# A hybrid attention layer on one core: scale and shift as columns made by one-column products, and the start stage reordered

## The chip, the cores and the metric

The kernel runs on one core of one Trainium2 chip. A core has a matrix engine (TensorE, PE in the profile, with its weight loads shown as PEld), VectorE (DVE), ScalarE (ACT), GpSimd (POOL) and SyncE (SP, which here only issues transfers). Each takes its own instructions in order; semaphores tie them together. The metric is the device time of one execution in microseconds (us), lower is better: the median of several runs.

## The reference

One decoder layer on x of 2048 rows by 1024. What matters here is the start: a conditioning vector c gives a shift, a scale and a gate of 1024 numbers each, and the normalised x is multiplied and moved by them before one wide input projection.

```python
mod = jax.nn.silu(c) @ w_ada[l] + b_ada[l]
shift, scale, gate = jnp.split(mod, 3, axis=-1)
h = rms_norm(x, g_pre[l]) * (1.0 + scale[:, None, :]) + shift[:, None, :]
proj = h @ w_in[l]
qa, ka, va, fa, za, qb, kb, vb, zb = jnp.split(proj, split_points, axis=-1)
oa = forgetting_attention(qa, ka, va, fa + b_fgate[l]) * jax.nn.silu(za)
ob = sliding_window_sink_attention(rope(qb), rope(kb), vb, sinks[l]) * jax.nn.silu(zb)
y = jnp.concatenate([oa, ob], axis=-1) @ w_out[l]
x = x + gate[:, None, :] * rms_norm(y, g_post[l])
```

(Reshapes are left out. `forgetting_attention` is causal softmax attention with a cumulative log gate, 8 heads of 64; the other is attention over a window of 128 with sinks.)

## The kernel before, in words

x is held as 16 blocks of 128 rows, x0 to x15, and four of them make a chunk (`ci` 0 to 3, 512 rows). For each chunk the kernel makes `hT[ci]`, the transposed, normalised, scaled and shifted x as two f16 parts, a high one and a low one, in 8 slices `k` of 128 columns. All projections are then three f16 products per slice (high by high, high by low, low by high) into one of three PSUM banks `bk`.

The start stage (lines 463 to 680) has to come before any of that:

- `load_ada(half, k)` loads one of 16 blocks of `w_ada`, 128x1024 f32, 512 KB: half 1 gives the scale, half 0 the shift. A ring of 8 buffers holds them, so half 0 waits until half 1 has been used. x0 to x3 are loaded behind the third block of half 0, x4 to x7 behind the last.
- The scale and the shift are needed as columns: number p of slice k in partition p, column k. Before, `silu(c)` is spread over 128 columns (`silb`) and is the stationary operand; a block of `w_ada` streams past it in two products of 512 columns (`ada_pe`), which gives the same row in all partitions. Four of the 16 blocks go over VectorE instead (`ada_dve`, multiply and add into `acc`), and `ada_sum` adds them in by a product with ones. `ada_col` picks the column out of the row by the identity and a reduction on VectorE.
- `squares(ci)` (ScalarE) and `root(ci)` make the inverse root of the mean square of each row; for chunk 0 the root is made on VectorE, for the others three instructions are on VectorE and the rest on GpSimd. `normal(ci)` multiplies the rows by it: on ScalarE for chunk 0, on VectorE for the others.
- A bound on |h| over all columns (`bmx`, then its maximum over the partitions) sets a power of two `pH`, and with it the final multipliers `Gp` and `Shp`.
- `turn(ci, k)` transposes slice k of the chunk's four blocks on TensorE; `scaled` (ScalarE, line 441) applies `Gp` and `Shp` to give the f32 slice `hf` and, for even k, the high part; `split` (VectorE, lines 445 and 446) makes the rest. Odd slices get their high part by a cast on VectorE.

Behind the start stage stands a list of units (`punits`, a slice number each): 8 units of the projection `kb` for chunk 0, then 8 of `vb`, then `zb0`, and so on; `fill` emits them in order, and `at_slice(n, f)` emits f just ahead of unit n. `kb` unit k needs both parts of `hT[0]` slice k. TensorE works through these units, and through all heads of attention behind them, in the order of the list.

Two things set the order in which instructions stand on an engine. Each engine keeps about the order of the code, but the framework puts single instructions earlier where it takes their inputs to be ready. A transfer whose buffer nothing has used before has nothing to wait for and can stand far ahead. Transfers from SP and ACT also share eight counters in turn: a transfer waits until the last one on its counter has landed (`DMAHW0` to `DMAHW7` in the rows below).

## Time and profile before

| | us |
|---|---|
| median of 3 runs (1157.06 to 1159.82) | 1157.67 |
| profiled execution, its own time | 1157.8 |
| its span, first to last instruction | 1156.1 |
| TensorE busy in it | 1116.8 (97%) |
| VectorE, ScalarE, GpSimd busy | 930.5, 661.4, 207.5 |

A row of the timeline gives the start, the length, the engine, the line of the code, what is written and read, how many instructions are merged, and in brackets the idle time before it with what ended that. Rows of stretches give the busy time of each engine, then TensorE's granted clock as a share of full speed, the busy share of the transfer engines, and GB/s. A product of f32 operands is shown as two records, a transpose as one.

### The profile page before, as it was taken

The page shows a single profiled execution, that of the slowest core. Times are in us where ns is not written, and L with a number is a line of the kernel's source. Part 1 is how long each engine was busy: PE and PEld are TensorE (multiplying, and loading weights), DVE is VectorE, ACT ScalarE, POOL GpSimd, SP SyncE. Part 2 cuts the span into 40 slices and gives each one's busy share as a digit, 9 for nine tenths or more (in the row PEclk, how much of TensorE's full clock was granted, in tenths as well). Part 3 has the DMA queues.
Part 4 walks back from the last instruction along what each step waited for, and adds up shares of the span by engine and source line. Part 5 has one row for each costly group of instructions (what it writes and reads, how often), then busy time and mean ns, then how long its engine had stood idle before and what let it go on. Part 6 is the DMA issues. An engine that isn't in the chain of part 4 may idle for free. (4 is left out here: it accounts for less than half of the span.)

```text
span 1156.1 us, 25291 instructions
## 1 busy us (share of the span) xinstructions
PE 1116.8 (97%) x9869; PEld 656.3 (57%) x9869; DVE 930.5 (80%) x2137; ACT 661.4 (57%) x1150; POOL 207.5 (18%) x332
## 2 busy tenths in 40 slices
PE   5899999999999999999999999999999999999997
PEld 2475544577765866555555555555555555544444
DVE  7877468987888568788988899888888887878885
ACT  2876344654555421666757666666776778534332
POOL 1122134554556530010010110001000000000000
PEclk9899999999999999999999999999999999999999
DMA  9943355433243232442344342123311337686743
GB/s 333 336 116 72 87 78 96 97 63 90 52 92 88 58 87 58 73 108 29 80 64 87 84 67 70 38 49 76 45 43 34 91 101 206 140 225 197 199 135 109
DMA packets 123476, 120.10 MB, mean 104 GB/s; under 512 B 64948, under 2 KB 100828, under 8 KB 123356
## 3 DMA queue, kind: packets, MB, share of 16 engines
q1 hardware_dynamic: 112088, 85.69, 27.6%
q0 software_dynamic: 10832, 32.50, 13.5%
q8 instruction: 77, 1.26, 0.6%
q14 instruction: 43, 0.35, 0.1%
q10 hardware_dynamic: 436, 0.28, 0.1%
HBM read 64.75 MB, written 25.18 MB: 78 GB/s over the span
## 5 line engine op out<-in xcount | busy, mean ns | idle before, releaser
L1356 ACT ACTIVATE p<-sta,lift,scl_qk 128x1024 f32<-128x1024 f32 (+2 forms) x160 | 172.0, 1075 | 131.6 <-PE sta L1350 82.6
L351 PE MATMUL bk<-hT,wh_qk 128*128 128x512 f16 x768 | 194.7, 378 | 0.0
L1363 DVE TENSOR_TENSOR pha<-p,pha 128x1024 f16<-128x1024 f32 (+2 forms) x160 | 169.1, 1057 | 0.2 <-ACT pha L1360 0.2
L1303 DVE TENSOR_REDUCE a_m<-bk 128x1 f32<-128x512 f32 x192 | 130.4, 686 | 45.8 <-PE bk L1300 44.8
L1576 PE MATMUL bk<-wohl,oz 128*128 128x512 f16 x744 | 165.3, 379 | 1.1 <-DVE oz L1525 0.7
L1360 ACT ACTIVATE pha<-p 128x1024 f16<-128x1024 f32 (+2 forms) x160 | 148.1, 926 | 5.9 <-PE poa L1376 1.2
L1576 PEld LDWEIGHTS <-oz 128*128 128x128 f16 x744 | 71.9, 99 | 82.8 <-DVE oz L1525 1.8
L1376 PE MATMUL poa<-vt,pha 128*128 128x65 f16 x1088 | 116.1, 192 | 1.4 <-DVE pha L1363 1.2
L1373 PE MATMUL poa<-vt,pha 128*128 128x65 f16 x1088 | 116.6, 193 | 0.8 <-DVE ona L1382 0.7
L1375 PE MATMUL poa<-vt,pha 128*128 128x64 f16 x1088 | 116.6, 194 | 0.0
L351 PEld LDWEIGHTS <-wh_qk 128*128 128x128 f16 x768 | 72.1, 97 | 74.4 <-issue 2.1
L1349 PE MATMUL sta<-T 128*128 128x512 f16 (+1 forms) x320 | 110.9, 346 | 2.8 <-ACT p L1356 2.7
L1300 PE MATMUL bk<-T 66*128 66x512 f16 (+2 forms) x320 | 109.7, 348 | 2.4 <-DVE a_m L1303 1.9
L1373 PEld LDWEIGHTS <-pha 128*128 128x128 f16 x1088 | 101.5, 96 | 15.5 <-DVE ona L1382 1.9
L1350 PE MATMUL sta<-T 69*128 69x512 f16 (+1 forms) x320 | 109.8, 348 | 0.0
L1375 PEld LDWEIGHTS <-pha 128*128 128x128 f16 x1088 | 100.9, 97 | 11.4
L1376 PEld LDWEIGHTS <-pha 128*128 128x128 f16 x1088 | 100.8, 99 | 1.8 <-DVE pha L1363 1.7
L351 PE MATMUL bk<-hT,wh_za 128*128 128x512 f16 x384 | 99.7, 378 | 0.0
L369 PE MATMUL bk<-wh_va,hT 128*128 128x256 f16 x768 | 91.9, 273 | 0.0
L351 PE MATMUL bk<-hT,wh_zb 128*128 128x512 f16 x384 | 91.6, 379 | 0.2 <-DVE qc L754 0.2
L351 PE MATMUL bk<-hT,wh_qb 128*128 128x512 f16 x384 | 91.2, 379 | 0.0
L369 PEld LDWEIGHTS <-hT 128*128 128x128 f16 x768 | 73.3, 98 | 12.2 <-issue 2.1
(459 smaller groups left out, 1919.7 us busy)
## 6 DMA issues: line engine op xcount, KB each, us to landing
hT<-in_x_dram SPq DMA_DIRECT2D x20, 512.0 KB
wa<-in_w_ada_dram SPq DMA_DIRECT2D x16, 512.0 KB
z_d<-tz POOLq DMA_DIRECT2D x32, 256.0 KB, 3.0
T<-z_d SPq DMA_DIRECT2D x16, 512.0 KB
T<-stq SPq DMA_DIRECT2D x62, 128.0 KB
out_dram<-hT SPq DMA_DIRECT2D x15, 512.0 KB
xt<-in_x_dram SPq DMA_DIRECT2D x12, 512.0 KB
qs<-qf SPq DMA_DIRECT2D x80, 64.0 KB
```

The source lines that it names most:

```text
L351: PE.matmul(ps, whl[:, a, k, :], hT[ci][:, b, k, :], start=(k == 0 and n == 0), stop=(k == KT - 1 and n == 2))
L369: PE.matmul(ps[:, (u % 2) * 2 * P:(u % 2 + 1) * 2 * P], hT[ci][:, a, k, u * P:(u + 1) * P], wv[p][:, b, k, :], start=(k == 0 and n == 0), ...
L1303: V.tensor_reduce(m3[:, u, pc:pc + 1], mx[:, :w], axis=AX.X, op=ALU.max)
L1349: PE.matmul(self.st[:, o:o + w], T[:, 3, kb_], T[:, 1, qc], start=True, stop=False)
L1350: PE.matmul(self.st[:, o:o + w], T[0:XR, 2, kb_], T[0:XR, 0, qc], start=False, stop=not diag)
L1356: A.activation(self.p32[:, :self.w], self.st[:, :self.w], AF.Exp, scale=scl[f"qk{self.hd}"][:], bias=lift[:])
L1360: A.activation(self.ph[:, 0, :self.w], self.p32[:, :self.w], AF.Copy)
L1363: V.tensor_tensor(self.ph[:, 1, :self.w], self.p32[:, :self.w], self.ph[:, 0, :self.w], op=ALU.subtract)
L1373: PE.matmul(po[:, u, :], ph[:, 0, pq], vt[:, b, hd, 0:65], start=(self.first and n == 0 and u == 0), stop=False)
L1375: PE.matmul(po[:, u, 0:64], ph[:, 0, pq], vt[:, b, hd, 65:VW], start=False, stop=False)
L1376: PE.matmul(po[:, u, :], ph[:, 1, pq], vt[:, b, hd, 0:65], start=False, stop=(self.last and n == len(self.blocks) - 1))
L1576: PE.matmul(py, self.hl[:, i, k, :], w_slot(8 * j + k)[:, cc], start=(k == 0 and m_ == 0), stop=(k == KT - 1 and m_ == 2))
```

## The change

The scale and the shift are made as columns at once: a 128x128 piece of a `w_ada` block is the stationary operand and the column of `silu(c)` the moving one, so one product gives 128 numbers of the result as one column (`ada_col(half, k)`: 8 such products per block, all 16 blocks on TensorE). `silb`, the two `acc` and VectorE's part are gone. The maximum of the bound over the partitions is made by one product of ones with a diagonal matrix `dgb` and one reduction, in place of a transpose, a reduction and a second product. Two of the four normalisations of chunk 0 go to VectorE. The squares of x6 and x7 move between the turned slices, and with them `root(1)` behind slice 4. The normalisations of chunk 1, two of which stood behind the start stage and two ahead of units 13 and 14, now all stand ahead of units (8, 9, 12, 13).

```diff
@@ normal
-            if ci == 0:
+            if ci == 0 and u < 2:
                 A.activation(xt[t], xt[t], AF.Copy, scale=r)
             else:
                 V.tensor_scalar(xt[t], xt[t], r, None, op0=ALU.mult)
@@ the start stage
-        silb = st.tile([P, KT, P], F32, name="silb")
-        V.tensor_copy(silb[:], sil[:].unsqueeze(2).broadcast_to([P, KT, P]))
-        pm = {1: [ps_x.tile([P, CH], F32, tag="x", name="pm") for _ in range(2)], 0: [bk[1], bk[2]]}
-        acc = [st.tile([P, D], F32, name=f"acc{n}") for n in range(2)]
-        def ada_mm(half, lhsT, rows_, begin, end):
-            for n in range(2):
-                PE.matmul(pm[half][n][:], lhsT, rows_[:, n * CH:(n + 1) * CH], start=begin, stop=end)
...
-        def ada_col(half, dst):
...
+        def ada_col(half, k):
+            for j in range(KT):
+                PE.matmul(bk[2 - half][:, j:j + 1], wa[half, k][:, j * P:(j + 1) * P], sil[:, k:k + 1],
+                          start=(k == 0 and j == 0), stop=(k == KT - 1 and j == KT - 1))
...
-        for k in (0, 1, 3, 4, 6, 7):
-            ada_pe(1, k, k == 0)
-        for k in (2, 5):
-            ada_dve(1, k, k == 2)
+        for k in range(KT):
+            ada_col(1, k)
...
-        ada_pe(0, 3)
-        ada_pe(0, 5)
+        for k in range(KT - 1):
+            ada_col(0, k)
         squares(0)
-        scl0 = col8("scl0")
-        ada_col(1, scl0)
+        scl1 = col8("scl1")
+        V.tensor_tensor(scl1[:], bk[1][:, 0:KT], cols[:, 24:32], op=ALU.add)
...
         root(0)
         normal(0)
-        ada_dve(0, 4, False)
-        ada_dve(0, 6, False)
-        ada_pe(0, KT - 1)
-        ada_sum(0, True)
         w_low("kb", 0, 1)
         w_low("vb", 0, 1)
-        turned = [turn(0, k) for k in range(5)]
-        squares(1)
-        shf0 = col8("shf0")
-        ada_col(0, shf0)
+        turned = [turn(0, k) for k in range(2)]
+        ada_col(0, KT - 1)
+        turned += [turn(0, k) for k in range(2, 4)]
+        squares(1, (0, 1))
         shf = col8("shf")
-        V.tensor_tensor(shf[:], shf0[:], cols[:, 16:24], op=ALU.add)
+        V.tensor_tensor(shf[:], bk[2][:, 0:KT], cols[:, 16:24], op=ALU.add)
...
         V.tensor_reduce(bmx[:], bnd[:], axis=AX.X, op=ALU.max)
-        PE.transpose(bk[0][0:1, 0:P], bmx[:], ident[:])
-        turned += [turn(0, k, bk[k - 4]) for k in (5, 6)]
-        bm = st.tile([1, 1], F32, name="bm")
-        V.tensor_reduce(bm[:], bk[0][0:1, 0:P], axis=AX.X, op=ALU.max)
-        PE.matmul(bk[0][:, P:P + 1], ones[0:1, :], bm[:], start=True, stop=True)
-        pow2_floor(pH[:], bk[0][:, P:P + 1], "p2t")
+        dgb = st.tile([P, P], F32, name="dgb")
+        V.tensor_scalar(dgb[:], ident[:], bmx[:], 1.0e-30, op0=ALU.mult, op1=ALU.max)
+        PE.matmul(bk[0][:, 0:P], ones[:], dgb[:], start=True, stop=True)
+        turned += [turn(0, 4)] + [turn(0, k, bk[k - 4]) for k in (5, 6)]
+        bm = st.tile([P, 1], F32, name="bm")
+        V.tensor_reduce(bm[:], bk[0][:, 0:P], axis=AX.X, op=ALU.max)
+        V.tensor_scalar(pH[:].bitcast(I32), bm[:].bitcast(I32), 0x7F800000, None, op0=ALU.bitwise_and)
...
-        V.tensor_scalar(pfl[:], ipH[:], 0.5, None, op0=ALU.mult)
-        root(1)
         for k in range(KT):
             turned[k][0]()
             turned[k][1]()
             if k == 0:
                 turned.append(turn(0, 7))
+                V.tensor_scalar(pfl[:], ipH[:], 0.5, None, op0=ALU.mult)
+            if k in (1, 3):
+                squares(1, (2 + k // 2,))
+            if k == 4:
+                root(1)
...
-        normal(1, (0, 1))
         spread(0)
@@ the list of units
-    for u in (2, 3):
-        at_slice(11 + u, lambda u=u: normal(1, (u,)))
+    for u in range(4):
+        at_slice((8, 9, 12, 13)[u], lambda u=u: normal(1, (u,)))
```

How the order moves on three engines follows; the number behind a name is that of the buffer.

SP at the very start of the program, before (`rows` are c, the gains and the biases, `wa10` is block 0 of half 1):

```order
L473 DMA rows_147<-in_c_dram 8x128 [waits DVE_49]
L474 DMA rows_147<-in_g_pre_dram 8x128
L475 DMA rows_147<-in_b_ada_dram 24x128
L480 DMA wa10_161<-in_w_ada_dram 128x1024
L480 DMA wa11_163<-in_w_ada_dram 128x1024 [waits DMAHW1_49]
```

SP at the same place, now (`xt12` is x12, a block of chunk 3):

```order
L410 DMA xt12_643<-in_x_dram 128x1024
L473 DMA rows_147<-in_c_dram 8x128 [waits DVE_49]
L474 DMA rows_147<-in_g_pre_dram 8x128
L475 DMA rows_147<-in_b_ada_dram 24x128
L480 DMA wa10_161<-in_w_ada_dram 128x1024 [waits DMAHW1_49]
L480 DMA wa11_163<-in_w_ada_dram 128x1024 [waits DMAHW2_49]
```

With `silb` and `acc` gone the buffer of x12 is one that the start stage does not use, and its load went from behind x11 to the first place. In the built program it holds counter 1, so the first block of `w_ada`, which waited for nothing, now waits until x12 has landed.

TensorE in half 0 of the scale and shift, before (`px` is a transposed slice, `acc0` the part from VectorE):

```order
L514 MATMUL bk1_137<-wa05_274,silb_198 128x512
L514 MATMUL bk2_138<-wa05_274,silb_198 128x512
L514 MATMUL bk1_137<-wa07_278,silb_198 128x512
L514 MATMUL bk2_138<-wa07_278,silb_198 128x512
L514 MATMUL bk1_137<-acc0_202,ones_125 128x512
L514 MATMUL bk2_138<-acc0_202,ones_125 128x512
L435 MATMUL px_378<-ident_116,xt0_262 128x128
```

TensorE at the same place, now:

```order
L507 MATMUL bk2_138<-sil_126,wa03_314 128x1 x8
L507 MATMUL bk2_138<-sil_126,wa04_316 128x1 x8
L507 MATMUL bk2_138<-sil_126,wa05_318 128x1 x8
L507 MATMUL bk2_138<-sil_126,wa06_320 128x1 x8
L435 MATMUL px_457<-ident_116,xt0_306 128x128
L435 MATMUL px_457<-ident_116,xt1_308 128x128
L435 MATMUL px_457<-ident_116,xt2_310 128x128
L435 MATMUL px_457<-ident_116,xt3_312 128x128
L435 MATMUL px_463<-ident_116,xt0_306 128x128
L435 MATMUL px_463<-ident_116,xt1_308 128x128
L435 MATMUL px_463<-ident_116,xt2_310 128x128
L435 MATMUL px_463<-ident_116,xt3_312 128x128
```

Blocks 4 and 6, which VectorE had, are on TensorE now, and the eight transposes of two slices stand ahead of block 7, whose eight products follow the last row.

VectorE in the turned slices of chunk 0, before (`hT0` and `hf` are the slices, `hT3` holds x4 to x7 at that time, `rst` is the inverse root of chunk 1; its three VectorE instructions stood ahead of the first slice):

```order
L446 TENSOR_TENSOR hT0_107<-hf_441,hT0_107 128x512 [waits Activation_49]
L445 CAST hT0_107<-hf_485 128x512 [waits Activation_49]
L446 TENSOR_TENSOR hT0_107<-hf_485,hT0_107 128x512 [waits DVE_49]
L672 TENSOR_REDUCE mxs_128<-wr_zb0_284 128x1 [waits DMAHW0_49]
L179 TENSOR_SCALAR kap_kb_508<-w_pw_321,pH_113 128x1
L179 TENSOR_SCALAR kap_vb_510<-w_pw_328,pH_113 128x1
L754 SCALAR_TENSOR_TENSOR qc_597<-bk0_136,cosT_111 128x512 [waits DMAHW5_49,DMAHW3_49,DMAHW7_49,DMAHW1_49,Activation_49]
L675 TENSOR_SCALAR kf_127<-kap_vb_510 128x1 [waits DVE_49]
L429 TENSOR_SCALAR hT3_110<-hT3_110,rst_409 128x1024 [waits DMAHW4_49,Pool_49]
L429 TENSOR_SCALAR hT3_110<-hT3_110,rst_409 128x1024
```

VectorE at the same place, now:

```order
L446 TENSOR_TENSOR hT0_107<-hf_511,hT0_107 128x512 [waits Activation_49]
L101 TENSOR_SCALAR rs_v_555<-ss_489 128x4
L106 TENSOR_SCALAR rs_h_558<-rs_v_555 128x4 [waits DVE_49]
L107 TENSOR_SCALAR rs_y_557<-rs_h_558 128x4 [waits DVE_49]
L445 CAST hT0_107<-hf_516 128x512 [waits Activation_49]
L446 TENSOR_TENSOR hT0_107<-hf_516,hT0_107 128x512 [waits DVE_49]
L446 TENSOR_TENSOR hT0_107<-hf_521,hT0_107 128x512 [waits Activation_49]
L429 TENSOR_SCALAR hT3_110<-hT3_110,rst_490 128x1024 [waits DMAHW5_49,Pool_49]
L445 CAST hT0_107<-hf_537 128x512 [waits Activation_49]
L429 TENSOR_SCALAR hT3_110<-hT3_110,rst_490 128x1024 [waits DMAHW6_49]
L446 TENSOR_TENSOR hT0_107<-hf_537,hT0_107 128x512 [waits DVE_49]
L634 TENSOR_REDUCE mxs_128<-wr_zb0_328 128x1 [waits DMAHW1_49]
```

The root of chunk 1 now begins behind slice 4, and the first two normalisations of chunk 1, the first of which waits for GpSimd, stand ahead of the cast and the low part of slice 7, where they had stood behind both.

21 lines of the change are left out of this document (removed).

## The prediction

> **What bounds the kernel now.** First the slices of the page and a table of stretches (columns: PE, PEld, DVE, ACT, POOL busy, TensorE's clock, share of the transfer engines, GB/s):
>
> ```profile
> PE   5899999999999999999999999999999999999997
> 0.00:20.00 20.00, 10.75 (x20) 4.15 (x21) 12.24 (x28) 4.68 (x8) 5.40 (x14) 1.00 0.88 300
> 20.00:40.00 20.00, 15.71 (x39) 6.73 (x38) 17.69 (x42) 13.80 (x21) 0.92 (x1) 0.91 1.03 406
> 60.00:70.00 10.00, 10.00 (x81) 7.32 (x79) 8.45 (x21) 7.81 (x14) 4.71 (x13) 1.00 0.38 90
> ```
>
> From 60 us on TensorE is the bound nearly without a break, so a delay at its first long run of products moves the end by as much. Up to 40 us the transfers are full, at 406 GB/s. The change lies wholly in this start. TensorE's timeline there:
>
> ```profile
> 6.67 3.39 PE L514 MATMUL pm<-wa,silb 128*128 128x512 f32 x4 [1.98 <-DMA wa<-in_w_ada_dram]
> 30.29 5.26 PE L514 MATMUL bk<-wa,silb 128*128 128x512 f32 x8 [3.97 <-DMA wa<-in_w_ada_dram]
> 35.88 1.98 PE L514 MATMUL bk<-wa,silb 128*128 128x512 f32 x4 [0.33 <-DMA wa<-in_w_ada_dram]
> 39.41 2.35 PE L435 MATMUL px<-ident,xt 128*128 128x128 f32 x20
> 45.69 0.38 PE L351 MATMUL bk<-hT,wh_kb 128*128 128x512 f16 x1 [1.90 <-ACT hT L441]
> 54.24 0.59 PE L351 MATMUL bk<-hT,wh_kb 128*128 128x512 f16 x2 [0.32 <-DVE hT L446]
> ```
>
> Three marks follow: block 3 of half 0 is there at 30.29 and block 7 at 35.88 (transfer); the turned slices begin on ScalarE behind `Gp` and `Shp`; `kb` of chunk 0 ends at 54.24 + 0.59 = 54.83. I measure the change by this last mark. Between the marks VectorE and ScalarE lead:
>
> ```profile
> 41.52 0.17 DVE L646 TENSOR_TENSOR shf<-shf,cols 128x8 f32<-128x8 f32 x1
> 42.12 0.16 DVE L652 TENSOR_REDUCE bmx<-bnd 128x1 f32<-128x8 f32 x1
> 42.65 0.28 DVE L657 TENSOR_REDUCE bm<-bk 1x1 f32<-1x128 f32 x1 [0.36 <-PE bk L654]
> 43.83 0.16 DVE L89 TENSOR_SCALAR p2t<-bk 128x1 f32<-128x1 f32 x1 [0.90 <-PE bk L658]
> 44.02 0.15 DVE L90 TENSOR_SCALAR pH<-p2t 128x1 int32<-128x1 int32 x1
> 44.74 0.16 DVE L101 TENSOR_SCALAR rs_v<-ss 128x4 f32<-128x4 f32 x1
> 45.14 0.17 DVE L107 TENSOR_SCALAR rs_y<-rs_h 128x4 int32<-128x4 int32 x1
> 50.36 0.72 DVE L446 TENSOR_TENSOR hT<-hf,hT 128x512 f16<-128x512 f32 x1 [0.18 <-ACT hf L441]
> 51.03 0.43 DVE L445 CAST hT<-hf 128x512 f16<-128x512 f32 x1
> 53.50 0.69 DVE L446 TENSOR_TENSOR hT<-hf,hT 128x512 f16<-128x512 f32 x1
> 56.17 1.40 DVE L429 TENSOR_SCALAR hT<-hT,rst 128x1024 f32<-128x1024 f32 x2
> ```
>
> ```profile
> 25.15 1.06 ACT L417 ACTIVATE junk<-xt 128x1024 bf16<-128x1024 f32 x1 [4.88 <-DMA xt<-in_x_dram]
> 26.49 1.06 ACT L417 ACTIVATE junk<-xt 128x1024 bf16<-128x1024 f32 x1 [0.20 <-DMA xt<-in_x_dram]
> 42.15 0.19 ACT L417 ACTIVATION_READ_ACCUMULATOR junk<-hT 128x1 f32 x1
> 44.86 0.78 ACT L441 ACTIVATE hT<-px,Shp,Gp 128x512 f16<-128x512 f32 x1 [2.53 <-DVE pfl L665]
> ```
>
> The reader sees 3.34 us from `shf` (41.52) to the first turned slice (44.86), which I call t, and 9.97 us from t to the end of `kb`.
>
> **Part 1, transfers.** x12 is loaded first, and block 0 of half 1 is issued only when it has landed. One 512 KB transfer takes 26.49 - 25.15 = 1.34 us, the lower bound of the delay. The upper one comes from the first block now:
>
> ```profile
> 2.22 0.36 SPq L480 DMA_DIRECT2D wa<-in_w_ada_dram  x1
> ```
>
> It was used at 6.67, 4.45 us behind its issue. If x12 is issued near 0.8 (an estimate: it stands ahead of the three small transfers that go first now) and takes as long, block 0 goes out at 5.25 in place of 2.22: 3.0 us late. In that gap the loads of `kb` and `vb` fill the engines, so I take 1.8, nearer the lower end: block 3 at 32.1, block 7 at 37.7. That x12 need not be loaded later costs and gives nothing I can see.
>
> **Part 2, one-column products.** A block is 8 products, 16 records. The nearest rows are a series of transposes, which load a 128x128 f32 operand each, and a lone one-column product with f32 weights:
>
> ```profile
> 39.41 2.10 PEld L435 LDWEIGHTS px<-ident,xt 128*128 128x128 f32 x19 [0.29 <-issue]
> 955.62 0.35 PEld L1514 LDWEIGHTS bk<-w_mx,ones 128*128 128x128 f32 x2 [0.18 <-ACT sv L1510]
> 955.78 0.28 PE L1514 MATMUL bk<-w_mx,ones 128*128 128x1 f32 x2
> ```
>
> 2.10 / 19 = 0.11 us a load, 1.8 us a block; 0.35 / 2 = 0.175 gives 2.8. The first is a series, as the blocks are, so I take 1.8. It is more than the 1.34 that a block takes to arrive. Half 1 does not bind: eight blocks and three of half 0 need 11 x 1.8 = 20 us between about 8.5 (6.67 + 1.8) and 32.1, with room for a slow first one. Then blocks 3 to 6 queue up: 32.1 + 4 x 1.8 = 39.3; eight transposes at 2.35 / 20 = 0.117 make 40.2; block 7, landed long before, ends at 42.0. With 0.1 to VectorE `shf` starts at 42.1, 0.6 later than now. At 1.3 a block it would be 36.4 + 1.3 + 0.9 + 1.3 + 0.1 = 40.0. VectorE's four `acc` blocks and the picking between the last product and `shf` are gone, but their place is taken by the queue on TensorE. Moving two normalisations of chunk 0 to VectorE ends them sooner and I cost it at nothing: the transposes that need them stand behind block 6, which ends at 39.3; without that cover (cheap columns) it would keep the 40.0 just given.
>
> **Part 3, the bound.** The second trip to TensorE (0.90) and `p2t` (0.19) go; `dgb` and a longer product come, 0.3 to 0.5. 3.34 becomes 2.65: t = 44.75, 0.1 earlier.
>
> **Part 4, the turned slices.** Two squares (1.06 + 0.19 each) stand in ScalarE's row now: 2.5 us. The low part of slice 4 ended near 51.03, t + 6.2; it ends at t + 8.7. Behind it come the three root instructions; L107 starts 0.4 behind L101, t + 9.1. GpSimd's part of such a root, in two places:
>
> ```profile
> 45.42 0.19 POOL L115 TENSOR_TENSOR rs_t<-rs_y 128x4 f32<-128x4 f32 x1
> 50.34 0.20 POOL L122 TENSOR_TENSOR rst<-rs_t,rs_y 128x4 f32<-128x4 f32 x1
> 96.54 0.48 POOL L115 TENSOR_TENSOR rs_t<-rs_y 128x4 f32<-128x4 f32 x1
> 100.44 0.20 POOL L122 TENSOR_TENSOR rst<-rs_t,rs_y 128x4 f32<-128x4 f32 x1
> ```
>
> 5.1 us beside a busy VectorE, 4.1 beside a calmer one. VectorE will mostly stand still, so 4.1: it starts 0.28 behind L107 and ends at t + 13.5. Only then can VectorE normalise x4, cast slice 7, normalise x5 and make the low part of slice 7 (1.40 for two, 0.43 and 0.69: 2.5). That is t + 16.1, and the last product ends at t + 16.4 where it ended at t + 9.97: 6.4 later. Queued behind VectorE are `kb`'s end on TensorE, `qf` and the squares of chunk 2 on ScalarE behind that, and `vb`. The normalisations themselves cost nothing more, since they only move ahead.
>
> **Part 5, the clock.** TensorE will stand nearly still from about t + 11 to t + 16. What such a pause does:
>
> ```profile
> 30.00:31.00 1.00, 0.71 (x1) 0.50 (x2) 0.90 (x7) 1.00 (x3) 0.00 (x0) 0.52 1.03 410
> 32.00:33.00 1.00, 1.00 (x2) 0.34 (x1) 0.90 (x4) 0.71 (x2) 0.00 (x0) 0.50 1.00 393
> 45.00:46.00 1.00, 0.31 (x1) 0.00 (x0) 0.28 (x2) 1.00 (x2) 0.63 (x4) 1.00 0.65 107
> ```
>
> After 3.97 us of idling the clock was 0.52 and 0.50 for some 3.4 us: up to 1.7 us lost if `vb` starts so, none if a window is missed or a later wait takes it up. I take 1.0.
>
> **Sum.** -0.1 + 6.4 + 1.0 = 7.3 us. The profiled execution took 1157.8, 0.1 above the median: 1165.1 against 1157.8, 1165.0 against 1157.67.
>
> **Rival A, slow columns.** A one-column product streams one column for each load, so TensorE may count as idle and stay at half clock. A cold pair of loads, against a warm one:
>
> ```profile
> 30.29 0.50 PEld L514 LDWEIGHTS bk<-wa,silb 128*128 128x128 f32 x2 [4.05 <-DMA wa<-in_w_ada_dram]
> 35.87 0.30 PEld L514 LDWEIGHTS bk<-wa,silb 128*128 128x128 f32 x2 [1.16 <-DMA wa<-in_w_ada_dram]
> ```
>
> 0.50 / 0.30 x 1.8 = 3.0 us a block (2.8 also if a load costs 0.175). Then transfers no longer matter: 8.5 + 16 x 3.0 + 1 = 57.5, `shf` 16 us late, less 0.7, and parts 4 and 5 come on top: +22.7, 1180; at 2.8 a block 1177. For it: no row here shows a long run of such products. Against it: 39.4 to 43.8 is transposes only, and the product at 45.69 still took 0.38 at a clock of 1.00. [...]
>
> **Rival B, not slower.** If GpSimd's root were done by t + 11, when VectorE comes to it, the wait in part 4 would vanish: `kb` ends 9.97 + 2.5 behind t, that is +2.5 - 0.1 = +2.4, 1160.1, within 0.3%. It decides at a root of 2 us; the rows show 4.1 and 5.1.
>
> **Chances.** The forecast with its own range of +3.5 to +11 (blocks at 1.3 or 2.2 us, root at 5.1): 0.60. Rival A: 0.26. Rival B: 0.10. The rest, a gain further on that takes the delay back: 0.04. The range reaches from B's 1160.0 to the lower half of A, 1178, and leaves out some 0.17. About 0.3% (3.5 us) is what a measurement of this kernel tells from no change: slower 0.83, the same 0.13 (B and the forecast's lowest end), faster 0.04.
>
> **What would show it.** Right: SP's first transfer is x12; some 0.11 us a load in line 507; ScalarE's first turned slice near 44.8; VectorE idle about 2 us ahead of L429 with GpSimd as releaser; `kb` ending near 61; a clock near 0.5 behind it. Wrong: a wait of TensorE for `w_ada` right up to block 7 (columns cheaper), L507 running far past 42 (rival A), or L429 without a wait (rival B).

## The result, and the profile after

The changed kernel takes 1200.52 us (median of 4, 1196.18 to 1206.95) against 1157.57 us: 1.0372 times as long, 95% interval 1.0343 to 1.0401, or 43.0 us more. The forecast was 1165.0 us, with a range up to 1178. The profiled execution took 1203.41 us, 45.6 more than the one shown of before.

The table of stretches of the changed kernel, with the columns of the prediction's first fence, shows TensorE and its loads busy without a break from 20 to 70 us while the other engines do next to nothing:

```profile
20.00:40.00 20.00, 20.00 (x95) 20.00 (x96) 2.62 (x3) 6.14 (x12) 0.00 (x0) 1.00 0.81 291
60.00:70.00 10.00, 10.00 (x49) 10.00 (x49) 0.00 (x0) 0.00 (x0) 0.00 (x0) 1.00 0.00 0
```

Its TensorE timeline (start, length, engine, line, operation, operands, count; in brackets the idle time before and what ended it):

```profile
12.81 27.44 PE L507 MATMUL bk<-sil,wa 128*128 128x1 f32 x128 [6.08 <-DVE kl L529]
41.62 24.05 PE L507 MATMUL bk<-sil,wa 128*128 128x1 f32 x112
67.28 3.41 PE L507 MATMUL bk<-sil,wa 128*128 128x1 f32 x16
70.55 1.95 PE L435 MATMUL px<-ident,xt 128*128 128x128 f32 x8
73.53 1.04 PE L435 MATMUL bk<-ident,xt 128*128 128x128 f32 x8
88.39 0.59 PE L351 MATMUL bk<-hT,wh_kb 128*128 128x512 f16 x1 [3.14 <-DVE hT L445]
89.66 1.01 PE L351 MATMUL bk<-hT,wh_kb 128*128 128x512 f16 x2 [0.68 <-DVE hT L446]
90.46 2.92 PE L756 MATMUL bk<-wh_vb,hT 128*128 128x136 f16 x24
```

A record of a one-column product takes 27.44 / 128 = 0.214 us, a block of 16 records 3.43 us, where the prediction had 0.11 and 1.8. The eight transposes at 70.55 take 1.95 us, and eight more, at 73.53, 1.04 us: up to 73 us what can be compared on TensorE ran at half rate. (The clock column reads 1.00 there; that is taken up at the end.) `kb` of chunk 0 ends at 89.66 + 1.01 = 90.67 against 54.83, 35.8 us later.

On SP, VectorE, ScalarE and GpSimd of the changed kernel the other marks of the prediction stand so:

```profile
0.79 0.41 SPq L410 DMA_DIRECT2D xt<-in_x_dram  x1
4.70 2.81 SPq L480 DMA_DIRECT2D wa<-in_w_ada_dram  x5
```

```profile
70.73 0.17 DVE L605 TENSOR_TENSOR shf<-bk,cols 128x8 f32<-128x8 f32 x1 [21.00 <-PE bk L507]
72.97 0.29 DVE L617 TENSOR_REDUCE bm<-bk 128x1 f32<-128x128 f32 x1 [1.15 <-PE bk L614]
87.25 0.75 DVE L429 TENSOR_SCALAR hT<-hT,rst 128x1024 f32<-128x1024 f32 x1 [2.69 <-POOL rst L122]
```

```profile
74.14 0.78 ACT L441 ACTIVATE hT<-px,Shp,Gp 128x512 f16<-128x512 f32 x1 [23.88 <-PE bk L435]
```

```profile
83.00 0.30 POOL L115 TENSOR_TENSOR rs_t<-rs_y 128x4 f32<-128x4 f32 x1
87.02 0.20 POOL L122 TENSOR_TENSOR rst<-rs_t,rs_y 128x4 f32<-128x4 f32 x1
```

The profile puts the wait ahead of 12.81 down to `kl`, which these products do not read; in the run with the columns alone below, where the first block is used at 12.46, the same wait is put down to that block's transfer.

`shf` comes at 70.73 instead of 41.52, and t at 74.14 instead of 44.86: 29.3 us for the columns and their late start. From t to the end of `kb` it is 16.53 us instead of 9.97: 6.6 us for the moved squares and root. `vb`'s first 24 products take 2.92 us at a clock of 0.50 (from 88 to 93 us, behind the pause of 3.14 us): 1.3 us more than before (1.58). That is 37.2 us, and by 462 us it is 35.5 (a little is taken up on the way). Then the changed kernel stops far behind its start, at a product that waits for a transfer into `T`, and runs slowly behind it:

```profile
462.32 0.22 PE L1261 MATMUL bk<-T 66*128 66x128 f16 x1
470.92 0.29 PE L1261 MATMUL bk<-T 66*128 66x128 f16 x1 [4.41 <-DMA T<-stq]
```

```profile
469.00:472.00 3.00, 1.08 (x4) 0.53 (x5) 0.76 (x3) 0.00 (x0) 0.55 (x1) 0.57 0.00 0
472.00:475.00 3.00, 3.00 (x9) 1.03 (x7) 1.32 (x4) 0.00 (x0) 0.54 (x1) 0.50 0.44 69
```

In the timeline of the kernel before the same two products stand at

```profile
426.83 0.22 PE L1300 MATMUL bk<-T 66*128 66x128 f16 x1
430.85 0.22 PE L1300 MATMUL bk<-T 66*128 66x128 f16 x1
```

without a wait: +35.5 us for the first, +40.1 for the second. The half clock behind the stop (0.50 from 472 to 475 us) and a second, shorter stop near 1001 us (shown further down) make most of what lies between 40.1 and the 45.6 us at the end. Three questions are left to the runs: what part of the change costs what, why a record takes 0.214 us, and where the last 6 to 10 us come from. "kb end" below is the end of the last `kb` product of chunk 0 in the run's profile, its start plus its length in TensorE's timeline, less 54.83.

### The profile page after: what moved, and what is told of

Read it like the earlier page. It is cut to its first block, busy times and chain, and to the rows that moved or that the text cites. A ratio compares the mean times of both kernels' runs of the same rounds, so it can differ in the third digit from the quotient of the medians.

```text
span 1201.7 us, 25688 instructions
## 1 busy us (share of the span) xinstructions
PE 1154.8 (96%) x10076; PEld 706.2 (59%) x10076; DVE 920.1 (77%) x2124; ACT 658.3 (55%) x1148; POOL 206.9 (17%) x332
## 3 DMA queue, kind: packets, MB, share of 16 engines
q8 instruction: 79, 1.29, 0.5%
## 5 line engine op out<-in xcount | busy, mean ns | idle before, releaser
L351 PE MATMUL bk<-hT,wh_qk 128*128 128x512 f16 x768 | 197.4, 382 | 0.0
```

The costliest lines, as they stand in the source:

```text
L351: PE.matmul(ps, whl[:, a, k, :], hT[ci][:, b, k, :], start=(k == 0 and n == 0), stop=(k == KT - 1 and n == 2))
```

## The experiments

### The parts alone

The kernel before with the one-column products only (`ada_col` of the change in place of `ada_pe`, `ada_dve` and `ada_sum`):

```diff
-        for k in (0, 1, 3, 4, 6, 7):
-            ada_pe(1, k, k == 0)
-        for k in (2, 5):
-            ada_dve(1, k, k == 2)
+        for k in range(KT):
+            ada_col(1, k)
...
-        ada_pe(0, 3)
-        ada_pe(0, 5)
+        for k in range(KT - 1):
+            ada_col(0, k)
```

> The one-column products alone (with the two scratch tiles that go with them), everything else in the order of the kernel before. Theory: the whole loss of this part is that a weight-load record of a one-column product takes 0.214 us, so the last shift column comes some 29 us later (70.73 us against 41.52 us), and behind it the turned slices run as before, so that the first product's last use of hT ends 10 us behind the first scaled slice and not 16.5 us. That gives about 1158 + 29 = 1187 us (1184 to 1192). Rival: the order of the squares and the root costs nothing once the columns are late, and all of the 43 us is the products': 1195 to 1202 us.

Measured: 1198.5 us (1192.71 to 1203.6), 1.0351 times before (1.0315 to 1.0387); kb end +31.1. The columns alone make the start 31 us late, near the theory's 29, but the end is 41.1 us late. That is the rival's number and not its reason: 10 us come behind the start.

The rest of the change without the one-column products (the changed kernel with `silb`, `ada_pe`, `ada_dve`, `ada_sum` and the old `ada_col` put back):

> The rest of the change alone: bound spread by one product, two of four x tiles normalised on DVE, squares and root of later x moved between the turned slices; the scale and shift come from the wide products of the kernel before. Theory (my steps 3 to 5): +7.3 us, 1163 to 1167 us; DVE waits some 2 to 3 us for the root before its first normalisation in the turned slices, and the products behind the pause run at half clock. Rival: the moved root hides once the columns are not late, 1157 to 1160 us. Second rival: what is behind the 37 us start in the changed kernel (some 8 us more by its end) belongs to this part, and it comes out at 1172 us or more.

Measured: 1165.67 us (1165.21 to 1166.36), 1.0070 (1.0055 to 1.0085), +8.2 us; kb end +7.0. On VectorE and TensorE of this run:

```profile
58.41 0.75 DVE L429 TENSOR_SCALAR hT<-hT,rst 128x1024 f32<-128x1024 f32 x1 [2.69 <-POOL rst L122]
```

```profile
61.62 2.62 PE L797 MATMUL bk<-wh_vb,hT 128*128 128x136 f16 x24
```

The wait for the root is there, 2.69 us as in the whole change, and `vb` starts slowly behind it. Here the theory holds, and nothing more is lost later.

The bound by one product, and two of chunk 0's normalisations on VectorE, alone:

```diff
-            if ci == 0:
+            if ci == 0 and u < 2:
...
-        PE.transpose(bk[0][0:1, 0:P], bmx[:], ident[:])
-        turned += [turn(0, k, bk[k - 4]) for k in (5, 6)]
+        dgb = st.tile([P, P], F32, name="dgb")
+        V.tensor_scalar(dgb[:], ident[:], bmx[:], 1.0e-30, op0=ALU.mult, op1=ALU.max)
+        PE.matmul(bk[0][:, 0:P], ones[:], dgb[:], start=True, stop=True)
+        turned += [turn(0, 4)] + [turn(0, k, bk[k - 4]) for k in (5, 6)]
```

> The kernel before with the bound spread by one product and two of the first four x tiles normalised on DVE; the columns, the squares, the root and the later normals stay as before. Theory (step 3 of the prediction): the first scaled slice comes 0 to 0.7 us earlier and DVE's two normals are hidden, so 1156.5 to 1158.5 us, and the 8.2 us of the run without the one-column products are all due to the moved root. Rival: the two normals on DVE or the later transposes cost, 1161 us or more, and the moved root costs correspondingly less.

Measured: 1157.45 us, 0.9999 (0.9989 to 1.0008). It is worth nothing either way, so by difference the 8.2 us of the run before belong to the moved squares, root and normalisations of chunk 1; no run takes these three apart.

### Why a record takes 0.214 us

Moving side of 64 equal columns (the scale vector's element repeated, a result of 64 columns each, of which the first is used):

```diff
+        silw = st.tile([P, KT, 64], F32, name="silw")
+        V.tensor_copy(silw[:], sil[:].unsqueeze(2).broadcast_to([P, KT, 64]))
...
-                PE.matmul(bk[2 - half][:, j:j + 1], wa[half, k][:, j * P:(j + 1) * P], sil[:, k:k + 1],
+                PE.matmul(bk[2 - half][:, j * 64:(j + 1) * 64], wa[half, k][:, j * P:(j + 1) * P], silw[:, k, :],
```

> The changed kernel, but each one-column product has 64 equal columns as its moving side (one f32 bank of 8 x 64 results, the first of each 64 is used). The loads are the same in number and size. Theory (half clock, because a record that streams one column leaves the array too idle): with 64 columns, some 0.054 us of streaming by the 0.43 us of a 512-column f32 record, the array is busy about half of the time, the clock rises, and a record takes 0.11 to 0.13 us: the shift columns come 20 to 25 us earlier, 1173 to 1182 us. Rival (0.214 us is what an f32 128x128 load with a product behind it takes at any clock): the record stays at 0.21 us or more and the time at 1196 to 1207 us.

Measured: 1198.29 us, 1.0332 (1.0296 to 1.0369); kb end +30.3. The theory's number missed:

```profile
6.53 3.65 PE L510 MATMUL bk<-silw,wa 128*128 128x64 f32 x16 [1.90 <-DMA wa<-in_w_ada_dram]
11.00 24.15 PE L510 MATMUL bk<-silw,wa 128*128 128x64 f32 x112 [0.82 <-DMA wa<-in_w_ada_dram]
```

A record still takes 24.15 / 112 = 0.216 us. By itself that speaks for the rival, that a load takes so long at any clock. (The tile `silw` changes how memory is laid out, and x12 is not loaded first here: the first block is used at 6.53 instead of 12.81, and half 1 is done at 35.15 instead of 40.25. So x12 in front cost some 5 us in the changed kernel, as far as this comparison goes.)

Dense records as a thermometer:

```diff
             for j in range(KT):
+                if j in (0, 4):
+                    PE.matmul(dum[:], ones[:], wa[half, k][:, 0:CH], start=True, stop=True)
                 PE.matmul(bk[2 - half][:, j:j + 1], ...
```

> The changed kernel with work added: in front of each four... eight-record half of a block one f32 product of 512 columns (two records) into a scratch bank that nobody reads, so four such records in each block of 16 one-column records. The dense records are the clock's thermometer: 0.43 us at full clock, 0.86 us at half. Theory (clock): the dense records lift the clock, they take 0.43 us and the one-column records near 0.11 us; a block takes 3.4 to 3.6 us, as before the addition, and the time stays near 1200 us although 64 records were added. Rival (a load with its product takes 0.214 us at any clock): dense 0.43 us, one-column 0.214 us, a block of 5.1 us, about 1228 us. If the clock stays low: dense 0.86 us, a block of 6.9 us, about 1255 us.

Measured: 1251.78 us, 1.0813 (1.0791 to 1.0834), the third case. TensorE's timeline:

```profile
14.51 1.71 PE L510 MATMUL bk<-sil,wa 128*128 128x1 f32 x8
16.07 2.05 PE L509 MATMUL dum<-wa,ones 128*128 128x512 f32 x2
17.92 1.71 PE L510 MATMUL bk<-sil,wa 128*128 128x1 f32 x8
...
119.83 0.95 PE L510 MATMUL bk<-sil,wa 128*128 128x1 f32 x8
```

From one row of eight to the next it is 17.92 - 14.51 = 3.41 us: two dense records of 0.85 and eight of 0.213. The dense ones too run at half rate (0.85 us; in the kernel before four such records from 22.31 have the next record at 24.02, 0.43 each), though they fill half of the time, 1.71 of the 3.41 us. At 119.83, behind 8 transposes and two dense records in a row, eight one-column records take 0.95 us, 0.119 each: the clock is up. So 0.214 is the half clock, not the load; the rival falls.

A warm-up of 48 records of 128 columns without a pause ahead of each half:

```diff
+        for _ in range(24):
+            PE.matmul(wup[:, 0:P], ones[:], ones[:], start=True, stop=True)
         for k in range(KT):
             ada_col(1, k)
```

> The changed kernel with work added: 24 f32 products of 128 columns (48 records that stream without a pause) into a scratch bank ahead of the first half's one-column products, and again ahead of the second half's, whose blocks have all landed by then. In the run with dense records added, eight one-column records took 0.95 us once 8 transposes and two dense records had stood in a row, so a one-column record can take 0.12 us. Theory A (a stretch of some 3.4 us without a pause in the streaming raises the clock, and one-column records then let it fall again): behind the warm-up some 28 to 32 records at 0.11 us, and the rest at 0.214 us; the time stays within 1198 to 1208 us. Theory B (once raised, the clock is held as long as TensorE has work): all 112 records of the second half at 0.11 to 0.12 us, 13 us in place of 24 us, and the first half done by 28 us instead of 40 us; about 1183 us (1178 to 1190).

Measured: 1203.63 us, 1.0395 (1.0372 to 1.0419): theory A. TensorE of the second half in the timeline, and in stretches of 1 us:

```profile
39.00 7.14 PE L585 MATMUL wup<-ones 128*128 128x128 f32 x48
45.98 21.10 PE L507 MATMUL bk<-sil,wa 128*128 128x1 f32 x112
```

```profile
42.00:43.00 1.00, 1.00 (x10) 1.00 (x10) 0.83 (x6) 0.31 (x1) 0.00 (x0) 0.90 1.04 426
48.00:49.00 1.00, 1.00 (x11) 1.00 (x11) 0.00 (x0) 0.00 (x0) 0.00 (x0) 1.00 1.13 211
49.00:50.00 1.00, 1.00 (x7) 1.00 (x6) 0.00 (x0) 0.00 (x0) 0.00 (x0) 0.52 1.08 221
```

The clock rises 3.2 us after the warm-up began (0.90 from 42 to 43 us, so near 42.2); the one-column records then run at 11 in a microsecond for 3 us, and fall back to 6 or 7 at 0.52 though TensorE never stops. What part of the time has to be streaming for the clock to rise, the two widths below narrow down.

Moving side of 128 columns (two PSUM banks a half), and the same with 96 of the 128:

```diff
+                PE.matmul(pm[half][j // 4][:, (j % 4) * P:(j % 4 + 1) * P], wa[half, k][:, j * P:(j + 1) * P],
+                          silb[:, k, :], start=(k == 0 and j % 4 == 0), stop=(k == KT - 1 and j % 4 == 3))
```

> The changed kernel, but every product's moving side is the scale vector's element repeated 128 times (the 128-column tile of the kernel before), so a record streams as long as its load takes; two PSUM banks a half, of which every 128th column is used. Theory (the low clock came from records that stream less than they load): the clock rises within some 4 us of the first blocks, a record takes 0.11 to 0.12 us, a block 1.8 to 2.0 us, below the 2.3 us in which a block lands, and the shift columns follow the last transfer: what is left is the order of squares and root (the run without the one-column products stood at 1165.7 us), so 1163 to 1172 us. Rival (the number of weight loads is what costs, at any clock): a record at 0.2 us or more, 1190 to 1200 us.

> As the run with 128 equal columns as the moving side, with 96 of the 128 used: a record then streams three quarters as long as its load takes. With 64 the clock stayed low (0.214 us a record), with 128 it rose (0.114 us). Theory (only streaming without a pause raises the clock): it stays low, a record takes 0.214 us, 1190 to 1200 us. Rival (a share of the time is enough, somewhere between a half and the whole): it rises, a record takes 0.11 to 0.12 us, 1170 to 1177 us.

Measured: 1174.77 us (1.0140, 1.0118 to 1.0161) with 128 columns, 1178.97 us (1.0178, 1.0147 to 1.0209) with 96. The second half's records in the two timelines:

```profile
27.13 12.77 PE L510 MATMUL bk<-silb,wa 128*128 128x128 f32 x112
40.61 1.95 PE L510 MATMUL bk<-silb,wa 128*128 128x128 f32 x16
```

```profile
26.97 12.74 PE L510 MATMUL bk<-silb,wa 128*128 128x96 f32 x112
```

12.77 / 112 = 0.114 us, in both. So in these runs it is a share of the time that counts, not a stream without a pause: at about half (64 columns, 0.216 us a record, or the dense records above, 0.85) the clock stayed low, at about three quarters (96 columns, 0.114) it rose. The shares of the two widths are estimates from the 0.43 us of a dense record: 64 columns are 0.43 x 64 / 512 = 0.054 us and 96 columns 0.081, against a record of some 0.11. For the 96 columns the theory is refuted; both times lie above what was expected of a raised clock (1163 to 1172 and 1170 to 1177 us). With the columns cured the start is 7.1 and 6.9 us late, what the run without them lost. For the 128 columns the sum of the prediction's Part 2 is right: block 7 ends at 40.61 + 1.95 = 42.6, and it had 42.0. But the ends are 16.5 and 21.6 us late, and again the difference lies behind the start.

### What is lost behind the start

The kernel before, delayed by 41 dense products ahead of its first transposes:

```diff
+        for _ in range(41):
+            PE.matmul(dum[:], ones[:], silb[:, 0:4, :], start=True, stop=True)
         turned = [turn(0, k) for k in range(5)]
```

> The kernel before with work added: 41 f32 products of 512 columns (82 records, 0.43 us each, 35 us) ahead of the first transposes, and nothing else. It asks for the part of the loss that lies behind the start: in the changed kernel's profile the first product that waits for a landed T stands 35.5 us later than before, and the end 45.6 us later. Theory (a late start alone makes later transfers meet other ones, so that waits and slow-clock stretches follow): 1198 to 1204 us, with a wait of some us for T in the trace. Rival (the further 8 to 10 us belong to the changed order): 1157.4 + 35 = 1191 to 1194 us.

The kernel before with 128-column products and everything else as it was (its start ends 0.4 us later than before):

> The kernel before with the scale and shift as 128-column products block by block (as in the run with 128 columns), and with bound, squares, root and normals in the order of before: the part of the change's idea without its clock and without its new order. Theory: a block takes 1.8 to 2.0 us and nothing of the columns is left on DVE, so the shift columns stand at 40 to 43 us, against 41.52 us before: 1155 to 1160 us, and if it is below 1157 us it beats both kernels. Rival (the loads are too many at any clock): 1185 us or more.

The delayed kernel before with 3 and with 9 dense products instead of 41:

> The kernel before with 3 f32 products of 512 columns (6 records of 0.43 us, 2.6 us) ahead of the first transposes, and nothing else. Three kernels showed the same wait for a landed T (4.4 to 5.0 us) with half clock behind it, one of them with no late start at all. Theory (the kernel before just misses this wait, and any other timing of its start can meet it): 1157.4 + 2.6 = 1160 us where it isn't met, 1167 to 1170 us where it is; a long issue (over 1.1 us) of the third transfer from stq some 9 us ahead of it would be seen with it. Rival (it needs a start that is tens of us later, or the wide products): 1159 to 1161 us in all runs.

> As the run with 3 added products, with 9 of them (18 records, 7.7 us). Theory (the wait is met or not by the timing of the start): 1157.4 + 7.7 = 1165 us where it isn't met, as in the run of the rest of the change alone (its start was as late, and it showed no such wait), 1172 to 1176 us where it is. Rival (a start of this lateness is always free of it): 1164 to 1166 us in all runs.

Measured: 1200.16 us (1.0353, 1.0327 to 1.0380) for the 41, 1167.4 us (1.0074, 1.0047 to 1.0101) for the 128 columns in the old order, 1163.19 us (1.0037, 1.0018 to 1.0056) for the 3 and 1171.38 us (1.0115, 1.0100 to 1.0130) for the 9. The 41 came out as the theory had it; the other three missed theory and rival alike (the 3 and the 9 lie between the two values of their theory). Neither a late start nor the new order is needed: the second kernel has the old order and a start only 0.4 us later, and it loses 9.1 us. In its TensorE timeline and on its SP:

```profile
434.74 0.29 PE L1266 MATMUL bk<-T 66*128 66x128 f16 x1 [4.96 <-DMA T<-stq]
```

```profile
425.23 1.64 SPq L1043 DMA_DIRECT2D T<-stq  x1
426.91 0.60 SPq L1044 DMA_DIRECT2D T<-stq  x1
```

One issue of a transfer takes 1.64 us instead of 0.60, and the product that needs its data starts 9.5 us behind it (4.4 us in the kernel before). In the changed kernel, with the columns alone, with the 96 columns and with the 41 dense products the pair is the same (issues of 1.2 to 1.7 us, 9 to 10 us to the product). With 9 dense products T comes in time, and the stop is in another place, at 165.11 us, where ScalarE's `stb` waits for VectorE and that for a transfer `qs` (with 3, the same product waits 1.73 us):

```profile
165.11 0.29 PE L892 MATMUL pss<-kst,stb 64*128 64x128 f16 x4 [3.41 <-ACT stb L771]
```

The queue list of the stretch from 425 to 426 us in the 128-column kernel shows what else is there (queue, packets, MB, share):

```profile
q1 hardware_dynamic: 174, 0.16, 67.9%
q8 instruction: 1, 0.02, 8.6%
```

And the pages of the kernel before and the changed one have for the whole execution

```profile
q8 instruction: 77, 1.26, 0.6%
```

```profile
PE 1154.8 (96%) x10076; PEld 706.2 (59%) x10076; DVE 920.1 (77%) x2124; ACT 658.3 (55%) x1148; POOL 206.9 (17%) x332
q8 instruction: 79, 1.29, 0.5%
```

1.29 MB / 79 is 16.3 KB a packet, and 2 x 10076 instructions of TensorE (products and loads) / 79 is 255 a packet, 2 x 9869 / 77 before 256. In all runs here the count follows TensorE's (77 packets up to 9887 products, 78 at 9951 and 9997, 79 from 10076). From the first packet to the last TensorE starts 19894 products and loads in the changed kernel, 255.1 for each of the 78 intervals, and 19368 before, 254.8 for each of 76. From these counts I take it that q8 brings TensorE's instructions, 256 at a time; no profile shows whose instructions a packet holds. The packets' place goes along with the stop. In six profiles with the stop at T (the changed kernel, the columns alone, the 96 columns, the 128 columns in the old order, the 41 dense products, and one below) a q8 packet lies in the same microsecond as that long issue. In the kernel before the nearest are at 416 and 442 us, the issue at 426. Over all 19 profiles, 84 of the 2356 issues of `T<-stq` take more than 1.1 us; a q8 packet starts between 1.0 us ahead of the issue's start and 0.6 us behind it for 61 of these 84, and for 209 of the other 2272.

A packet at that place is not enough for the stop, though. The changed kernel with 64 columns and the one with 128 have it within half a microsecond of the same issue,

```profile
464.58 1.18 SPq L1042 DMA_DIRECT2D T<-stq  x1
434.27 0.98 SPq L1046 DMA_DIRECT2D T<-stq  x1
```

and no product of theirs waits 2 us for T. They too lose time later, like the other six, at a product of `w_mx`. Its wait in the changed kernel:

```profile
1001.01 0.38 PE L1475 MATMUL bk<-w_mx,ones 128*128 128x1 f32 x2 [1.65 <-ACT sv L1471]
```

In these eight profiles this product waits 0.8 to 2.2 us. In the other eleven it does not wait, and no product waits over 1.3 us for T.

If q8 brings TensorE's instructions, the packets' place in the program depends on how many instructions TensorE has had: the change adds 207 products and as many loads, 414 instructions, 158 beyond one whole packet; this remainder is called the phase below. So the next runs shift this phase and nothing else, by products of one by one element in pauses of TensorE at the start:

```diff
+        for _ in range(24):
+            PE.matmul(tin[0:1, 0:1], ones[0:1, 0:1], ones[0:1, 0:1], start=True, stop=True)
         PE.transpose(bk[0][:, :P], rows[:], ident[:])
```

Added to the 128-column kernel in the old order (416 + 96 = 512):

> The kernel before with the scale and shift as 128-column products, and the same 24 small products ahead (416 + 96 = 512 instructions, two whole packets). Theory: without the shift this kernel loses only what its start loses, 0.4 us: 1157 to 1159 us in place of 1167.4 us. Rival: 1165 to 1169 us.

Added to the kernel delayed by 41 products (23 small ones, 256):

> The kernel before with 35 us of products ahead of the first transposes, as in the earlier run, and 23 small products (164 + 92 = 256 instructions, one whole packet). Theory: the late start alone costs what it is long, 34.4 us at kb's last product: 1191 to 1193 us in place of 1200.2 us. Rival: 1199 to 1202 us.

Added to the kernel before, which puts it out of phase (41 small ones, 164):

> The kernel before with 41 of the small products (164 instructions), 24 ahead of the first transpose and 17 in the pause ahead of block 3 of half 0, so that its start stays as it is but the instruction transfers move by 164, as in the run with 35 us of products added. Theory: the waits of that run appear without its late start, 1164 to 1169 us, T landing 4 to 5 us late in the profile. Rival: 1157 to 1160 us.

Added to the changed kernel (510, and with one bf16 product more 512):

> The changed kernel with 24 f32 products of one by one element ahead of TensorE's first transpose, where it stands idle: 48 records, 96 instructions, into a scratch bank. TensorE's instructions come in by transfers of 256 of them (79 packets of 16 KB in the profile); the change adds 414 instructions to TensorE's start, which moves each of these transfers by 158 instructions of 256 against the program. In the profiles in which T lands late such a transfer lies in the same microsecond as the third transfer from stq, and in the kernel before it does not. With 96 more the shift is 510, 2 short of two whole packets. Theory: the transfers stand against the program as in the kernel before, the waits behind the start go, and only what the start costs is left: 35.8 us to kb's last product and 1.4 us of half clock, 1193 to 1196 us. Rival (the late landings have nothing to do with the instruction transfers): 1198 to 1203 us.

> The changed kernel with 24 f32 and one bf16 product of one by one element ahead (98 instructions), so that the shift of the instruction transfers is 512, two whole packets, and not 510 as in the run before. That run lost its waits for T, but TensorE stood without instructions for 3.48 us at 863 us, behind an instruction transfer at 853 us. Theory (these stops belong to where the instruction transfers fall, and two instructions can decide at a tight place): no stop of over 2 us behind the start, 1193 to 1196 us. Rival (with the late start such a stop comes somewhere in any case): 1198 to 1203 us.

Measured, with the instructions added to TensorE ahead of the start's end, the phase they leave (of 256), the start's delay in the one profiled execution, and the median less that of before in the same comparison:

| kernel | added | phase | kb end, us | time, us | time less kb end |
|---|---|---|---|---|---|
| changed | 414 | 158 | +35.8 | +43.0 | 7.2 |
| changed, 98 more | 512 | 0 | +35.1 | +36.7 | 1.6 |
| changed, 96 more | 510 | 254 | +35.5 | +40.7 | 5.2 |
| columns alone | 416 | 160 | +31.1 | +41.1 | 10.0 |
| 64 columns, new order | 414 | 158 | +30.3 | +40.9 | 10.6 |
| 96 columns, new order | 414 | 158 | +6.9 | +21.6 | 14.7 |
| 128 columns, new order | 414 | 158 | +7.1 | +16.5 | 9.4 |
| 128 columns, old order | 416 | 160 | +0.4 | +9.1 | 8.7 |
| the same, 96 more | 512 | 0 | +1.3 | +0.7 | -0.6 |
| before, 41 dense | 164 | 164 | +34.4 | +41.9 | 7.5 |
| the same, 92 more | 256 | 0 | +34.6 | +33.5 | -1.1 |
| before, 164 more | 164 | 164 | +0.8 | +8.1 | 7.3 |
| before, 3 dense | 12 | 12 | +1.9 | +5.8 | 3.9 |
| before, 9 dense | 36 | 36 | +7.2 | +14.0 | 6.8 |
| rest of the change alone | -2 | 254 | +7.0 | +8.2 | 1.2 |
| bound alone | -2 | 254 | -0.1 | 0.0 | 0.1 |

Four of the five came out as the theory had it: 1158.78 us (1.0003, 0.9992 to 1.0014), 1191.53 us (1.0286, 1.0262 to 1.0310), 1166.17 us (1.0070, 1.0043 to 1.0096) for the kernel before out of phase, and 1195.27 us (1.0323, 1.0306 to 1.0341) for the changed kernel at 512. The two kernels with 41 dense products start within 0.2 us of each other and end 8 us apart, so there it is not the start's time that decides. The kernel before out of phase has the stop, the changed one in phase does not; their timelines:

```profile
441.12 0.24 PE L1306 MATMUL bk<-T 66*128 66x128 f16 x1 [5.10 <-DMA T<-stq]
```

```profile
466.96 0.22 PE L1267 MATMUL bk<-T 66*128 66x128 f16 x1
```

(The profile of the kernel before out of phase is its slowest of seven executions, 1161.26 to 1171.69 us, and also has the stop at `stb`, 3.14 us at 156.34. At phase 0 the executions lie closer: 1190.76 to 1192.84 us for the delayed kernel, 1194.41 to 1195.64 for the changed one.)

The fifth, at 510, missed, and its time is the rival's: 1198.79 us (1.0343, 1.0318 to 1.0368), three executions near 1198.8 and one at 1194.75. Its long waits for T are gone, but in its profile TensorE stands once for nothing that the profile shows, and goes on 9 us behind a q8 packet:

```profile
863.15 0.19 PE L1337 MATMUL poa<-vt,pha 128*128 128x65 f16 x1 [3.48 <-issue]
```

That it lacked instructions there, as the expectation for 512 has it, is argued from this, not shown; the changed kernel at 512 has a packet and a long issue (3.65 us) at the same place, 855 us, and does not stop. The rest of the change alone has the same phase and no such stop, so the phase decides together with what else is under way. The 3 and the 9 dense products lose theirs at `stb`, ahead of T, and no run tells whether their phase or their later start does that.

The kernels with 128 and 96 columns in the new order (phase 158) belong with the bad ones: 16.5 and 21.6 us for a start 7 us late; neither was run at phase 0. That the phase costs most of these 6 to 10 us is shown in both directions, in three kernels by taking it away and in one by adding it. How a packet of 16 KB would delay another transfer by some 5 us, while the transfer engines are idle for much of it (0.00 from 469 to 472 us above), is not known. No kernel here beats the one before.

## Why the prediction was wrong

**Part 2 is the step that failed.** "2.10 / 19 = 0.11 us a load, 1.8 us a block ... The first is a series, as the blocks are, so I take 1.8." The transposes were the nearest row in what they load, and the wrong one in what they stream: 128 columns for each load, and one here. A record took 0.214 us and a block 3.43. Sixteen blocks then need 54.9 us, with the late start (12.8) and the eight transposes and two small products between them 70.7: `shf` at 70.73, not 42.1. Of the 43.0 us 29 are this, some 5 of them by way of the late start (Part 1 below), and the term was +0.6. Rival A named the mechanism, half clock, and put it at 3.0 us a block by 0.50 / 0.30; the ratio of 0.214 to 0.11 would have been 2, as the rows at 30.00 (0.52) and 45.00 (1.00) of the clock column had it. It had a chance of 0.26. What stood against it, that transposes hold a clock, says nothing of a record that by an estimate streams for a hundredth of its time (0.85 us / 512 = 0.0017 us of its 0.214). "Transfers no longer matter" was right.

**Transposes and the clock.** The prediction set against rival A that an f16 product behind transposes takes its full-clock time; it does so too where a half clock stands ahead of the transposes. In the run with the columns alone 29 transposes, with two small records behind them, follow the cold columns, and the first f16 product behind them takes what it takes at full clock:

```profile
68.59 4.51 PE L435 MATMUL px<-ident,xt 128*128 128x128 f32 x20
76.83 0.38 PE L351 MATMUL bk<-hT,wh_kb 128*128 128x512 f16 x1 [1.90 <-ACT hT L441]
```

(0.38 as at 45.69 before; 0.59 where the clock is at half, as for the same product at 88.39 in the changed kernel.) So the clock rose behind f32 transposes of 128 columns here. (The stretch from 39.4 to 43.8 that the prediction set against the rival is not transposes alone: the last two records, at 43.41, are a product.)

**Part 1** was too low as well: block 0 of half 1 is issued at 4.70 instead of 2.22 and used at 12.81 instead of 6.67, 6.1 us later where 1.8 was taken and 3.0 was the bound. With TensorE as the bound of the columns 5 us of this reached the end (35.15 against 40.25 for half 1); at full clock it would nearly have hidden by the sum of Part 2 (12.81 + 11 x 1.8 = 32.6, against block 3 at 32.1), which no run shows.

**Part 3**: 3.41 us from `shf` to t, not 2.65. The chain itself did become shorter (2.84 us, 45.30 - 42.46, in the run without the columns); in the changed kernel `dgb`'s product stood behind eight transposes at half clock, the 1.15 us of waiting ahead of L617. Alone it moved the time by nothing.

**Part 4** was right: `kb` ends at t + 16.53, foretold t + 16.4; GpSimd's root took 87.22 - 83.00 = 4.2 us, foretold 4.1; VectorE waited 2.69 us for it at L429, foretold about 2. **Part 5** was right: half clock behind the pause, 1.3 us for 1.0. Together they are the 8.2 us of the run without the columns, for the 7.3 of the sum. **Rival B** did not come about.

**Not in the prediction at all**: the 414 instructions as such. Every part was priced by what it does in its own place, and "a delay at its first long run of products moves the end by as much" was the premise of the sum. It holds for the late start at phase 0 (34.6 us at `kb`, 33.5 at the end) and not in the changed kernel (35.8 and 43.0). What the number of instructions does behind the start, worth 43.0 - 36.7 = 6.3 us here (read as a shift of each later instruction transfer against the program), was in no term and no rival. In the words of the range: rival A with the right price and the right start, 29.3 + 6.6 + 1.3, ends at 1195, and the phase makes it 1200.

## What to carry to other kernels

Price a matrix instruction by what it streams, not only by what it loads: here a series of products with one moving column ran at half clock for all of its 58 us (0.214 us a record, from 12.81 to 70.69, TensorE busy without a break from 20 to 40 us), and the transposes among it took double (1.95 us for eight, 1.04 behind it); the same series with 96 or 128 equal columns took 0.114 us a record, and its start was 6.9 and 7.1 us late, as without the columns. When an edit adds or removes some hundred instructions of one engine, a few microseconds at quite another place may change with it, as here 8.1 us with 164 small instructions in pauses; before explaining them by the edit, shift the phase by instructions that do nothing, in a pause, and look again. And a change that moves work between stalls (the squares and the root, into a row whose end another engine waits for) is paid in full when that wait is on the path: 16.5 us for 10.

## What the runs showed of the hardware that was not expected

In the changed kernel the clock column says 1.00 from the start of the execution up to 87 us, and so for 60 us in which every record that can be compared took twice its time; in the kernel before it says 1.00 at 6.67 too, where four dense records take 3.39 us, 0.85 each. Where a change has been recorded it agrees with the records (0.90 and 0.52 in the warm-up run, 0.50 at 88.39 in the changed kernel). A record's own length is the safer sign: 0.214 or 0.114 us for a 128x128 f32 load.

The share of streaming that raised the clock lies between about a half and three quarters (64 columns or dense records half of the time: never in 50 and 100 us, 0.216 and 0.213 us a record; 96 columns: within some 5 us of a series, 0.114 us a record). Once up, one-column records let it fall after 3 to 4 us (3.1 and 4.2 in the warm-up run), though TensorE has no gap.

The kernel before stands at a phase that happens to be good, or nearly so: of the kernels tried, those at 0 lose up to 2 us behind `kb`, those at 254 between 0 and 5, and those at 158 to 164 lose 7 to 15. Those at 12 and 36 lose 4 and 7, for which the phase is not shown to be the cause.
